# Output projection of a decoder layer: columns 0 to 1023 as seven block products of quarters, columns 1024 to 2047 first, token sums made beside those

## The chip, the core and the metric

The kernel runs on one core of one Trainium2 chip. The time is device microseconds (us) of one execution. The kernel before took 1541.53 us (median of 3 runs, 1541.39 to 1544.05). One execution was profiled; all rows below come from it.

Five engines matter. PE multiplies matrices; each matmul here holds a 128x128 block (the stationary operand, loaded just ahead of it) and streams the other operand past it into a PSUM bank, 512 columns wide or 256. DVE and ACT work element by element, on SBUF and on PSUM. SP and POOL issue transfers; a transfer that POOL issues may add to what lies in SBUF already. Each engine takes its instructions in the order in which the program lists them for it, and waits at the head of that list until what the instruction needs is there.

## The reference, cut to what matters

```python
x: (1, 512, 2048) f32;  w_out: (2048, 2048) f32
merged = sigmoid(g_mla) * y_mla + sigmoid(g_sgu) * y_sgu      # (1, 512, 2048)
x = x + gate[:, None] * (merged @ w_out)                      # one output projection
return rmsnorm(x, final_norm_g)                               # over the 2048 columns of a token
```

Everything ahead of these lines (adaLN, the input projection, attention over 16 heads, the spatial gating unit) is the same in both kernels.

## The kernel before, in words

All products are made in three matmuls: each f32 operand is cut into a high part (rounded to the matmul's f32r format) and a low part (the rest), and a product is high x high + high x low + low x high (`mm3`, L185 to L187; `block` and `out_block` do the same).

`merged` lies transposed in SBUF as 16 chunks of 128 channels x 512 tokens, in high and low parts, `mh[j]` and `ml[j]` (tiles `b0` to `b15` and `g0` to `g15`). `w_out` is cut into four column groups of 512 (cg 0 to 3) and each of these into 8 granules of 256 channels (`wo[cg, i]`, a tile of 128 x 1024, 512 KB).

A `Stream` (`ws`) brings the granules, in the order of its list:
- `dma_to` has SP load a granule into one of three raw tiles, `wraw0` to `wraw2`, and holds back when all three are held; a raw tile is given back when its granule has been split.
- `cast_to` has ACT copy it into a high tile (L139, `w0h` or `w1h`); `split_to` has DVE subtract the high part from the raw one into a low tile (L151, `w0l` or `w1l`). A high and a low tile of a granule can be overwritten only when PE has done the granule two places earlier.
- `get(i)` is called at the start of a step: it puts the cast and the split of granule i+1 on the lists of ACT and DVE, and returns granule i. What a step does besides stands behind them on the same lists.

The output projection is a row of 32 such steps. The first three (cg 0, i = 0 to 2) are worked in between the parts of attention's last head. A step (`out_granule`) is 24 matmuls of 512 columns: 2 chunks x 4 token blocks of 128 x 3. The four token blocks of a column group lie in four PSUM banks; the next group takes the other four. When a group is done, `residual` runs for its four token blocks, one per `get`: DVE multiplies by the gate row (`grow`) and adds the input (`yt`), ACT squares the row into a sum (L1838), DVE multiplies by the final norm's gain (`gfb`).

In cg 2, each `get` also brings a granule of cg 3 into tiles of its own (`dh`, `dl`), so that at the end cg 3 can be worked token block by token block: 48 matmuls of 512 columns for each of the first three blocks, and for the last one 48 of 256 columns twice. Each block's row is finished and stored while the next is multiplied: sum of squares, square root (ACT L1869), reciprocal, scale, four stores of 256 KB.

Earlier stages of the same kernel make two other projections as seven products of quarters in place of eight (`block`, L701, for 512, 384 or 320 columns; and L1502 to L1504). There, sums of weights are made by transfers that add (`onto`, L284, `transfer`, L866) or by DVE.

Of the kernel before, what the change touches and what calls it, by code (L numbers as in the profile page):

```python
# [20 lines left out]
P = 128  # L21
D = 2048
# [143 lines left out]
def trunk_layer(ctx, tc, xT, xn, c, vecs, pos, wada, w1, w2, wv, wv3, wv4, wh, wh15, wq, wqr, wk, wvv, wo, wsT, bsp, gfin, out,  # L166
# [188 lines left out]
    dlast = []  # L355

    def last_tiles():
        k = len(dlast)
        dlast.append((nt(dp[0].p, [P, GW], F32R, f"dh{k}"), nt(dp[0].p, [P, GW], F32R, f"dl{k}")))
        return dlast[-1]  # L360

    go = {}
    for cg in range(3):
        for i in range(8):
            go[cg, i] = ws.add(wo[cg, i], GW)
            if cg == 2 and i < 6:
                go[3, i] = ws.add(wo[3, i], GW, to=last_tiles)
    for i in (6, 7):
        go[3, i] = ws.add(wo[3, i], GW)
# [551 lines left out]
    for s in range(n_slots):  # L921
        def both(s=s):
# [5 lines left out]
        on(s - 2, SPLIT, both)  # L928
# [840 lines left out]
    def out_granule(cg, i, banks, ahead=1):  # L1769
        wH, wL = get(go[cg, i], ahead)  # L1770
# [7 lines left out]
    for h in range(H):  # L1778
# [5 lines left out]
        first = go[0, 0] if not more else gr[pair] if not odd and 2 * pair < H else None  # L1784
# [6 lines left out]
        else:  # L1791
            pso = [bank_at(k) for k in range(NB)]
            for i in range(2):
                out_granule(0, i, pso)
# [3 lines left out]
        if more:  # L1798
            kps = kproj(h + 1)
            kfinish(h + 1, kps)  # L1800
        else:
            merge()
            out_granule(0, 2, pso)
# [18 lines left out]
    grow = nt(dp[0].p, [P, D], F32, "gbc")  # L1822
    gfb = nt(dp[0].p, [P, D], F32, "gfb")
    yt = nt(dp[0].p, [P, NB, D], F32, "y")
    load_before(go[0, 7], lambda: (DMA.dma_start(grow, bcast(gate_row, D)), DMA.dma_start(gfb, bcast(gfin, D))))
    for n in range(NB):
        load_before(go[1, n], lambda n: DMA.dma_start(yt[:, n], xn[n]), n)
    ssy = nt(dp[0].p, [P, NB, 5], F32, "ssy")
    ry = nt(dp[0].p, [P, 12], F32, "ry")

    def residual(n, part, sl, ps, last=False):
        y = yt[:, n, sl]
        w = sl.stop - sl.start
        t = nt(tp, [P, S], F32, "sig", bufs=3)[:, :w]
        tt(t, ps, grow[:, sl], ALU.mult)
        tt(y, t, y, ALU.add)
        junk = nt(tp, [P, S], F32, "sig", bufs=3)[:, :w]
        ACT.activation(junk, y, AF.Square, accum_out=ssy[:, n, part:part + 1])  # L1838
        if not last:
            tt(y, y, gfb[:, sl], ALU.mult)  # L1840

    for cg in range(3):
        if cg > 0:
            pso = [bank_at((4 * cg + k) % 8) for k in range(NB)]
# [107 lines left out]
```

## Time and profile before

| | |
|---|---|
| median of 3 runs | 1541.53 us |
| the profiled execution | 1542.18 us, of which the span from its first to its last instruction is 1540.5 us |
| granted TensorE clock, mean | 0.999 |
| matmuls in the program | 10533 |
| ACT's cast in the first step of cg 1 / of cg 2 starts at | 1401.16 us / 1444.68 us |
| last matmul starts at | 1532.04 us |
| transfers that add, all before 1056 us | 58.2 MB in 111 of 512 or 384 KB and some small ones |

The page's first part gives for each engine its busy time and share of the span. The timeline lists instructions in order of time: start, duration, engine, line, operation, output<-inputs, shape, and in brackets how long the engine sat idle before it and what ended that. A matmul's duration is its way through the array; the next one starts before it is over.

### The profile page before, as it was taken

How to read it: one execution, taken by the hardware profiler on the slowest of the kernel's cores; microseconds unless marked ns; L12 is line 12 of the kernel's file. 1: busy time of each engine (PE TensorE's matmuls, PEld its weight loads, DVE VectorE, ACT ScalarE, POOL GpSimd, SP SyncE). 2: the span in 40 equal slices, each digit the busy share in tenths (PEclk: the TensorE clock that was granted, in tenths of full speed). 3: DMA queues.
4: the chain of work that ended last, by engine and by line, in shares of the span. 5: the costliest groups of instructions: out<-in, count | busy, mean ns of one | idle time of the engine just before them, and what ended most of it. 6: DMA issues, size and time to landing. Idle time of an engine off the chain costs nothing.

```text
span 1540.5 us, 27351 instructions
## 1 busy us (share of the span) xinstructions
PE 1527.4 (99%) x10632; PEld 1423.8 (92%) x10632; DVE 1194.3 (78%) x1856; ACT 784.8 (51%) x1379; POOL 112.0 (7%) x136
## 2 busy tenths in 40 slices
PE   9999999999999999999999999999999999999997
PEld 7888988999999999999999999999888888888886
DVE  8989988768888888877777777778788888854543
ACT  4444566555555454454546546456555555632322
POOL 0000011011111111111101111120000000000000
PEclk9999999999999999999999999999999999999999
DMA  9978699778999998998888888887544443245423
GB/s 376 389 270 313 194 266 295 226 210 235 283 248 268 276 252 255 262 240 231 216 239 248 216 244 242 217 200 209 175 131 134 127 138 133 89 164 181 139 80 110
DMA packets 134868, 335.97 MB, mean 218 GB/s; under 512 B 15417, under 2 KB 39761, under 8 KB 130001
## 3 DMA queue, kind: packets, MB, share of 16 engines
q1 hardware_dynamic: 116434, 275.76, 51.8%
q0 software_dynamic: 18160, 58.20, 20.8%
q8 instruction: 83, 1.36, 0.3%
q14 instruction: 47, 0.39, 0.1%
q10 hardware_dynamic: 144, 0.26, 0.0%
HBM read 310.24 MB, written 23.94 MB: 217 GB/s over the span
## 4 chain that ended last, share of the span: by engine, by line
PE 94%; DMA 3%; ACT 1%; DVE 1%; issue 1%; SPq 0%; DVEq 0%; ACTq 0%; POOL 0%; POOLq 0%
PE ps L1502 15%; PE ps L1503 15%; PE ps L1504 15%; PE ps L186 12%; PE ps L185 12%; PE ps L187 12%; PE ps L701 7%; PE ps L1681 1%; DMA wraw<-in_wv 1%; PE ps L1062 1%; DMA wraw<-in_w 1%; PE ps L1645 1%; PE ps L1644 1%; DMA half<-in_pos 0%; DMA raw<-in_wv 0%
## 5 line engine op out<-in xcount | busy, mean ns | idle before, releaser
L1502 PE MATMUL ps<-h,w0h 128*128 128x256 f32 x408 | 113.1, 277 | 0.9 <-DVE lat L173 0.9
L1502 PE MATMUL ps<-h,w2h 128*128 128x256 f32 x408 | 113.8, 279 | 0.0
L1504 PE MATMUL ps<-h,w0l 128*128 128x256 f32 x408 | 112.7, 276 | 0.0
L1503 PE MATMUL ps<-h,w0h 128*128 128x256 f32 x408 | 112.7, 276 | 0.0
L1504 PE MATMUL ps<-h,w2l 128*128 128x256 f32 x408 | 112.7, 276 | 0.0
L1503 PE MATMUL ps<-h,w2h 128*128 128x256 f32 x408 | 112.7, 276 | 0.0
L1502 PE MATMUL ps<-h,w1h 128*128 128x256 f32 x400 | 110.9, 277 | 0.0
L1504 PE MATMUL ps<-h,w1l 128*128 128x256 f32 x400 | 110.5, 276 | 0.0
L1503 PE MATMUL ps<-h,w1h 128*128 128x256 f32 x400 | 110.5, 276 | 0.0
L139 ACT CAST w0h<-wraw 128x1024 fp32r<-128x1024 f32 (+5 forms) x67 | 59.1, 889 | 73.3 <-PE ps L187 25.3
L151 DVE TENSOR_TENSOR w0l<-wraw,w0h 128x1024 fp32r<-128x1024 f32 (+5 forms) x61 | 63.7, 1047 | 38.6 <-ACT w0h L139 38.1
L173 DVE TENSOR_TENSOR w0l<-raw,w0h 128x1024 fp32r<-128x1024 f32 x56 | 68.5, 1224 | 31.2 <-ACT w0h L888 30.4
L139 ACT CAST w1h<-wraw 128x1024 fp32r<-128x1024 f32 (+5 forms) x67 | 53.9, 811 | 72.4 <-PE ps L187 25.0
L151 DVE TENSOR_TENSOR w1l<-wraw,w1h 128x1024 fp32r<-128x1024 f32 (+5 forms) x63 | 59.1, 943 | 36.9 <-ACT w1h L139 33.9
L185 PE MATMUL ps<-h,w1h 128*128 128x512 f32 x218 | 86.6, 397 | 0.0
L186 PE MATMUL ps<-h,w1h 128*128 128x512 f32 x218 | 85.1, 390 | 0.0
L187 PE MATMUL ps<-h,w1l 128*128 128x512 f32 x218 | 85.0, 390 | 0.0
L173 DVE TENSOR_TENSOR w1l<-wraw,w1h 128x1024 fp32r<-128x1024 f32 x44 | 53.9, 1225 | 36.4 <-ACT w1h L888 36.4
L173 DVE TENSOR_TENSOR w2l<-wraw,w2h 128x1024 fp32r<-128x1024 f32 x46 | 56.3, 1224 | 30.2 <-ACT w2h L888 30.2
L185 PE MATMUL ps<-h,w0h 128*128 128x512 f32 x198 | 78.1, 394 | 0.0
L186 PE MATMUL ps<-h,w0h 128*128 128x512 f32 x198 | 77.3, 390 | 0.5 <-DVE h L176 0.5
L1502 PEld LDWEIGHTS ps<-h,w0h 128*128 128x128 f32 x408 | 76.6, 188 | 1.0 <-issue 1.0
(419 smaller groups left out, 5461.6 us busy)
## 6 DMA issues: line engine op xcount, KB each, us to landing
raw<-in_wh SPq DMA_DIRECT2D x104, 512.0 KB, 6.9
wada<-in_wada SPq DMA_DIRECT2D x31, 1024.0 KB, 7.7
wraw<-in_wh POOLq DMA_DIRECT2D x55, 512.0 KB, 8.3
wraw<-in_wh SPq DMA_DIRECT2D x44, 512.0 KB, 6.4
raw<-in_wh POOLq DMA_DIRECT2D x36, 512.0 KB, 7.4
wraw<-in_wo SPq DMA_DIRECT2D x32, 512.0 KB, 3.6
half<-in_w SPq DMA_DIRECT2D x35, 256.0 KB, 5.4
wraw<-in_w SPq DMA_DIRECT2D x16, 512.0 KB, 8.4
```

The lines of the kernel that those rows point to most:

```text
L139: self.nc.scalar.copy(self.hi[k][0][:, sl], src)
L151: self.nc.vector.tensor_tensor(out=lo[:, sl], in0=src, in1=hi[:, sl].bitcast(F32), op=ALU.subtract)
L173: DVE.tensor_tensor(out=out, in0=in0, in1=in1, op=op)
L185: PE.matmul(ps, ah, bh, start=start, stop=False)
L186: PE.matmul(ps, ah, bl, start=False, stop=False)
L187: PE.matmul(ps, al, bh, start=False, stop=stop)
L701: PE.matmul(psv[key][n], x_[:, tk], w_[:, sl], start=st and m == 0, stop=ch == 7 and m == 2, skip_group_check=True)
L1062: PE.matmul(ps[:, n], v[:, n], wr[:, q], start=True, stop=True)
L1502: PE.matmul(ps[:, :256], wH[:, cols[c]], xh, start=c == 0 and first, stop=False, skip_group_check=True)
L1503: PE.matmul(ps[:, :256], wH[:, cols[c]], xl, start=False, stop=False, skip_group_check=True)
L1504: PE.matmul(ps[:, :256], wL[:, cols[c]], xh, start=False, stop=c == 7, skip_group_check=True)
L1644: PE.matmul(ps, q2[:, q], krh[:, :n], start=False, stop=False)
```

## The change

Columns 1024 to 2047 (cg 2, then cg 3) now come first, in 16 steps as before (steps 0 to 15 below). Columns 0 to 1023 and the 512 tokens and 2048 channels are cut in halves each way, and the eight products of quarters are replaced by seven, named "1" to "7". Each is 8 chunks x 2 token blocks x 3 = 48 matmuls of 512 columns, in four steps of 12 (`out_block`):

| steps | product | stationary: tokens | weights: quarters of `wo[0]`, `wo[1]` |
|---|---|---|---|
| 16 to 19 | "1" | `mh`, left half | `wo[1, i]`, loaded |
| 20 to 23 | "6" | V, right half | `wo[0, i]` + `wo[1, i]`, added by a transfer in tile `ch` |
| 24 to 27 | "7" | V, left half | `wo[1, 4+i]`, loaded |
| 28 to 31 | "2" | U, left half | `wo[1, 4+i]` added onto `ch` |
| 32 to 35 | "3" | U, right half | `wo[1, i]` loaded, `wo[1, 4+i]` added onto it |
| 36 to 39 | "4" | `mh` of chunks 8 to 15, right half | `wo[0, 4+i]` added onto `ch` |
| then | "5" | `mh` of chunks 8 to 15, left half | `wo[0, 4+i]`, loaded; token blocks 0 and 1, the second in two halves of 256 columns |

(The signs and the exact quarters are those of the code; a granule's number in a tile's name is 144 + step, so `w1h_162` is step 18.)

- The token sums U and V are made by `out_sums(j)`, one per step, at steps 4 to 7 and 12 to 15: two DVE additions of 512 columns, four subtractions or additions of 256, an ACT copy and a DVE subtraction for V's high and low part. `split_u(j)` cuts U into high and low parts at steps 18 to 23.
- Products share two pairs of banks: "1", "2", "3", "4" add up in y; "6" and "7" in z. Between them, ACT copies a bank out (`hold`, L1889): z after step 23, y after steps 31 and 35. The four corners of the result are put together by DVE from these copies (`difference`, `corner_row`, `c11`, `c21`).
- `plain_row` is the old `residual` for cg 2 (steps 8 to 11) and cg 3 (steps 16, 17, 26, 27); the multiplication by the gain stands apart (`weigh`).
- From step 18 the stream has a third high tile (`w2h`) and casts two granules ahead; the low tiles stay two. From step 16 it looks seven granules ahead for loads.
- Rows 2 and 3 are finished by `row_out` (two ACT multiplications of 1024 columns, two stores of 512 KB), rows 0 and 1 by the old end.

The diff, cut to what is spoken of:

```diff
+    def chain_out(i):
+        chain[i] = t = nt(dp[0].p, [P, GW], F32, f"ch{i}")
+        DMA.dma_start(t, wo[0, i])
+    go = {(cg, i): ws.add(wo[cg, i], GW) for cg in (2, 3) for i in range(8)}
+    for p in "1672345":
+        for i in range(2 if p == "5" else 0, 4):
...
+            elif p == "3":
+                g = ws.add(wo[1, i], GW, fetch=lambda t, i=i: both(t, wo[1, 4 + i]))
+            elif p == "6":
+                g = ws.add(None, GW, fetch=lambda t, i=i: [chain[i][:, :]])
+            else:
+                src, by = wo[int(p == "2"), 4 + i], go["6" if p == "2" else "2", i]
+                g = ws.add(None, GW, fetch=lambda t, i=i, src=src: chain_add(i, src, GW), after=by)
...
+    def out_sums(j):
...
+        tt(u, mh[j].bitcast(F32), ml[j].bitcast(F32), ALU.add)
+        tt(v, mh[j + 8].bitcast(F32), ml[j + 8].bitcast(F32), ALU.add)
+        tt(v[:, right], u[:, right], v[:, right], ALU.subtract)
+        tt(u[:, right], u[:, left], u[:, right], ALU.subtract)
+        tt(u[:, left], v[:, right], u[:, left], ALU.subtract)
+        tt(v[:, left], u[:, left], v[:, left], ALU.add)
+        V[j] = nt(dpp, [P, 2, S], F32R, f"V{j}")
+        hilo(V[j][:, 0], V[j][:, 1], v)
...
+    def hold(name, n, ps, pl, tag):
+        held[name, n] = t = nt(pl, [P, S], F32, tag, bufs=3 if tag == "sig" else 1)
+        ACT.copy(t, ps)
...
+    for n in range(2):
+        at_out(23, lambda n=n: hold("z6", n, pbank["z"][n], dpp, f"k{n}"))
+        at_out(31, lambda n=n: hold("y12", n, pbank["y"][n], tp, "sig"))
+        at_out(35, lambda n=n: hold("y123", n, pbank["y"][n], tp, "sig"))
+    for j in range(8):
+        at_out((4, 5, 6, 7, 12, 13, 14, 15)[j], out_sums, j)
+        at_out((18, 18, 19, 19, 20, 21, 22, 23)[j], split_u, j)
+    for n in range(NB):
+        at_out(8 + n, plain_row, n, 2)
+        at_out((16, 17, 26, 27)[n], plain_row, n, 3)
...
+        if s == 16:
+            ws.look = 7
+        if s == 18:
+            a, b = ws.next_hi, 1 - ws.next_hi
+            ws.his, ws.next_hi = [(dpp, "w2h", 0, 0), ws.his[a], ws.his[b]], 0
...
+            w = get(seq[s], cast=seq[s + 2] if s >= 18 else None)
...
+                out_block(p, i, n, w, pbank[key][n])
+        for f in todo.pop(s, ()):
+            f()
```

**How it moves instructions, place one: ACT around step 16.** Before, at the same place (the start of cg 2) ACT's list has two casts in a row, then a square (`w0h_162` is the granule two steps on, `dh1` one of cg 3):

```order
L139 CAST dh0_2005_16497<-wraw1_161_16407 128x1024
L139 CAST w0h_162_16501<-wraw2_162_16437 128x1024
L1838 ACTIVATE sig_2008_16512,ssy_1987_16067<-y_1986_16066 128x512
L139 CAST dh1_2009_16539<-wraw0_163_16467 128x1024
L139 CAST w1h_164_16543<-wraw1_164_16505 128x1024
```

Now, from step 13's `get` to step 18's (V5 to V7 are the high parts of token sums, `ps4` and `ps5` the squares of `plain_row`, `b0` the high part of a split U):

```order
L139 CAST w1h_158_16464<-wraw1_158_16353 128x1024
L190 CAST V5_2018_16501<-sig_2017_16494 128x512
L139 CAST w0h_159_16505<-wraw2_159_16390 128x1024
L190 CAST V6_2021_16543<-sig_2020_16536 128x512
L139 CAST w1h_160_16547<-wraw0_160_16426 128x1024
L190 CAST V7_2023_16584<-sig_2022_16577 128x512
L139 CAST w0h_161_16588<-wraw1_161_16468 128x1024
L1896 ACTIVATE ps4_2002_16270,ssy_1984_16064<-yp_1991_16071 128x512
L139 CAST w1h_162_16612<-wraw2_162_16509 128x1024
L1896 ACTIVATE ps5_2003_16271,ssy_1984_16064<-yp_1991_16071 128x512
L139 CAST w2h_163_16634<-wraw0_163_16551 128x1024
L139 CAST w0h_164_16638<-ch0_2006_16278 128x1024
```

Between two casts there now stands one instruction that needs DVE's work of the step before.

**Place two: POOL and ACT around steps 32 to 37.** Before, POOL issues nothing in the output projection. Now its list ends with 16 transfers that add; the last eight are those of steps 32 to 39:

```order
L284 DMA wraw2_176_16788<-in_wo 128x1024
L284 DMA wraw0_177_16814<-in_wo 128x1024
L284 DMA wraw1_178_16836<-in_wo 128x1024
L284 DMA wraw2_179_16933<-in_wo 128x1024
L284 DMA ch0_2006_16278<-in_wo 128x1024
L284 DMA ch1_2008_16314<-in_wo 128x1024
L284 DMA ch2_2010_16351<-in_wo 128x1024
L284 DMA ch3_2012_16388<-in_wo 128x1024
```

`wraw2` serves step 32 (176) and again step 35 (179), so the load and the added transfer of 179 come after the split of 176, and those onto `ch0` to `ch3` stand behind them on POOL. ACT's list at steps 33 to 37 (`sig_2064`, `sig_2065` are the copies of the y banks after step 35):

```order
L139 CAST w0h_179_16986<-wraw2_179_16933 128x1024
L1896 ACTIVATE ps4_2036_16690,ssy_1984_16064<-ys0_2040_16708 128x512
L139 CAST w1h_180_17007<-ch0_2006_16278 128x1024
L1896 ACTIVATE ps5_2037_16691,ssy_1984_16064<-ys1_2041_16710 128x512
L139 CAST w2h_181_17026<-ch1_2008_16314 128x1024
L1889 COPY sig_2064_17040<-ps0_2024_16594 128x512
L1889 COPY sig_2065_17042<-ps1_2025_16595 128x512
L139 CAST w0h_182_17048<-ch2_2010_16351 128x1024
```

The copies of the y banks, which step 36 writes next, now stand behind the cast of step 37's granule.

**Place three: ACT at the end.** Before, between the square of row 2 and the two half squares of row 3 stand a square root and one multiplication of 512 columns, both of row 2. Now, behind the square of row 0 (`sig_2074`), two multiplications of row 3 stand ahead of the half squares of row 1 (`sig_2075`, `sig_2076`):

```order
L1896 ACTIVATE sig_2074_17169,ssy_1984_16064<-ys0_2040_16708 128x512
L2026 ACTIVATE ry_1985_16065<-ssy_1984_16064,ry_1985_16065 128x1
L2034 ACTIVATE yp_1991_16071<-yp_1991_16071,ry_1985_16065 128x512
L1947 ACTIVATE yp_1991_16071<-yp_1991_16071,ry_1985_16065 128x1024
L1947 ACTIVATE ys3_2063_16980<-ys3_2063_16980,ry_1985_16065 128x1024
L1896 ACTIVATE sig_2075_17212,ssy_1984_16064<-ys1_2041_16710 128x256
L1896 ACTIVATE sig_2076_17243,ssy_1984_16064<-ys1_2041_16710 128x256
```

More of the change, by code (lines that the diff above doesn't have):

```diff
@@ L1842, in trunk_layer @@
[L1842 to L1851 removed]
+    dpp = dp[0].p
+    ssy = nt(dpp, [P, NB, 5], F32, "ssy")
```

223 lines of the change are left out of this document (158 added, 65 removed).

## The prediction, made before the changed kernel was run

> **What bounds the kernel now.** I read the page's busy times first, then the chain that ended last, then who PE waited for.
>
> ```profile
> span 1540.5 us, 27351 instructions
> PE 1527.4 (99%) x10632; PEld 1423.8 (92%) x10632; DVE 1194.3 (78%) x1856; ACT 784.8 (51%) x1379; POOL 112.0 (7%) x136
> PE 94%; DMA 3%; ACT 1%; DVE 1%; issue 1%; SPq 0%; DVEq 0%; ACTq 0%; POOL 0%; POOLq 0%
> PE ps L701 <- DVE w1l L151: 1.4, 1, 1.4
> 1444.40:1532.30 87.90, 87.90 (x434) 74.59 (x432) 44.14 (x67) 27.14 (x45) 0.00 (x0) 1.00 0.32 108
> ```
>
> PE has no room: 94% of the closing chain is matmuls, and the longest of its waits on other work is 1.4 us, for one split. The last row is the stretch from cg 2 to the last matmul: PE busy throughout, DVE 44.14 and ACT 27.14 of 87.9 us. So fewer matmuls shorten the kernel as long as DVE, ACT and the transfers keep up. By their totals they would. The question is the order.
>
> **What goes: matmuls.** Not the mean duration counts but the distance between starts:
>
> ```profile
> 1505.00 0.39 PE L185 MATMUL ps<-dh,b 128*128 128x512 f32 x1
> 1520.42 0.39 PE L187 MATMUL ps<-w0h,g 128*128 128x512 f32 x1
> 1520.64 0.28 PE L185 MATMUL ps<-dh,b 128*128 128x256 f32 x1
> 1532.04 0.28 PE L187 MATMUL ps<-w0h,g 128*128 128x256 f32 x1
> ```
>
> From the first to the second lie 68 distances: 15.42/68 = 0.227 us. From the third to the fourth 95: 11.40/95 = 0.120 us. Before: 720 matmuls of 512 columns and 96 of 256; after: 384 + 288 + 24 = 696 and 48. Gone are 24 x 0.227 + 48 x 0.120 = **-11.2 us**. (By the durations, 0.39 and 0.28, it would look like some 23.) A step of 24 takes 5.44 us, one of 12 takes 2.72.
>
> **What comes, first term: ACT's line at steps 12 to 19.** Durations of the pieces:
>
> ```profile
> 1401.16 1.05 ACT L139 CAST w0h<-wraw 128x1024 fp32r<-128x1024 f32 x1 [4.38 <-PE ps L187]
> 1402.25 1.23 DVE L151 TENSOR_TENSOR w0l<-wraw,w0h 128x1024 fp32r<-128x1024 f32 x1 [4.22 <-ACT w0h L139]
> 1403.39 0.68 DVE L173 TENSOR_TENSOR sig<-ps,gbc 128x512 f32<-128x512 f32 x1
> 1404.11 0.69 DVE L173 TENSOR_TENSOR y<-sig,y 128x512 f32<-128x512 f32 x1
> 1404.83 0.63 ACT L1838 ACTIVATE sig<-y 128x512 f32<-128x512 f32 x1 [2.62 <-DVE y L173]
> 1448.36 0.63 ACT L1838 ACTIVATE sig<-y 128x512 f32<-128x512 f32 x1 [2.62 <-DVE y L173]
> 1448.99 1.03 ACT L139 CAST dh<-wraw 128x1024 fp32r<-128x1024 f32 x1
> 1344.62 0.68 DVE L151 TENSOR_TENSOR w0l<-wraw,w0h 128x512 fp32r<-128x512 f32 x1
> 1345.23 1.49 DVE L173 TENSOR_TENSOR lat<-ps,lat 128x512 fp32r<-128x512 f32 x3
> 194.98 0.42 DVE L173 TENSOR_TENSOR x<-x,x 128x256 f32<-128x256 f32 x1
> 195.43 0.42 DVE L173 TENSOR_TENSOR x<-x 128x256 f32<-128x256 f32 x1
> 1532.81 0.43 DVE L173 TENSOR_TENSOR y<-sig,y 128x256 f32<-128x256 f32 x1
> 1533.27 0.42 ACT L1838 ACTIVATE sig<-y 128x256 f32<-128x256 f32 x1 [5.25 <-DVE y L173]
> 1370.72 0.62 ACT L190 CAST b<-sig 128x512 fp32r<-128x512 f32 x1 [1.36 <-DVE sig L173]
> 1371.24 1.05 ACT L139 CAST w0h<-wraw 128x1024 fp32r<-128x1024 f32 x1
> ```
>
> From start to start: cast to split 1.09, split to the next DVE operation 1.14, 512 columns to a dependent operation 0.72, to an independent one 0.61, 256 columns to a dependent one 0.45 (to ACT 0.46), ACT's cast of 512 to its next 0.52, its square to its next cast 0.63.
>
> With token sums (steps 12 to 15) one turn is: split 1.14, first sum 0.61, second 0.72, three of 256 columns 1.35, the fourth and over to ACT 0.46, high part of V 0.52, next cast and over to DVE 1.09: 5.89 us, against a step of 5.44. The cast of step s+1 stands behind the high part of V, so the turn runs 0.45 us late per step. A nominal split starts 1.29 us into a step (the cast 0.2 in, 1.09 more). Step 12's is nominal; three turns on, that of step 15 starts 2.64 in, and step 16's (granule 17) 3.09 in. PE wants that low part at 2.72 + 0.23 = 2.95; it is there at 3.09 + 1.23 + 0.03 = 4.35: PE waits 1.4. In steps 16 and 17 the turn is split 1.14, `plain_row` 0.72 + 0.72, square 0.63, cast 1.09 = 4.30 us, but a PE step that starts on its low part takes 2.72: 1.58 more, twice. Then the casts run two ahead and nothing of this stands between. **+4.5 us.** If nothing is late at step 16, 2.9 remain. Steps 4 to 7 run late in the same way, but steps of 5.44 us follow and take it up.
>
> **Second term: steps 24 and 32.** A copy of z's second bank starts 0.2 into step 24; behind it on ACT stands the high part of the last U (0.52 on), for which DVE waits (0.65), and then come `weigh` (0.61), the next operation (0.61) and only then the split of granule 25: start 2.59, there at 3.85 against 2.95: **+0.9 us**. At step 32 the same with a cast of 1024: the split of 33 is there at 4.2, +1.3; this one is counted in the next term.
>
> **Third term: steps 31 to 36, a raw tile that comes free late.**
>
> ```profile
> wraw<-in_wo SPq DMA_DIRECT2D x32, 512.0 KB, 3.6
> raw<-in_wh POOLq DMA_DIRECT2D x36, 512.0 KB, 7.4
> 205.78 1.88 POOL L284 DMA_DIRECT2D raw<-in_wv  x2 [196.11 <-DMA raw<-in_wv]
> 209.25 0.85 POOL L284 DMA_DIRECT2D raw<-in_wv  x1 [0.18 <-issue]
> DMA to landing us min/median/max: 9.2/12.0/14.5
> 308.03 0.84 POOL L284 DMA_DIRECT2D raw<-in_wv  x1 [5.37 <-DVE w0l L151]
> 310.11 0.85 POOL L284 DMA_DIRECT2D raw<-in_wv  x1 [1.24 <-DVE w1l L151]
> DMA to landing us min/median/max: 4.8/5.0/5.1
> ```
>
> Let R be the start of step 31. Granule 35 needs the raw tile of 32, whose split ends at R + 1.9. Its load lands 3.6 later (R + 5.5), and only then may POOL add the second quarter; the transfers of granules 36 to 39 wait behind that on POOL. An added transfer takes a. In the rows: 7.4 in the median of a busy stage; 9.2 to 14.5 for a burst of four issued from 205.78 to 209.25, beside other traffic; 4.8 to 5.1 for one from 308.03 on. I take a = 7.4, as loads run beside it here as well. The first burst, issued within 3.5 us, landed from 215.0 to 223.75, so g = 8.75/3 = 2.9 us apart. Granule 37 then lands at R + 5.5 + a + 2g. ACT's cast of it (0.96 to the next) stands ahead of the copy of the y banks (0.6), which PE's step 36 waits for: R + 7.05 + a + 2g, where R + 13.6 is nominal. So the delay is a + 2g - 6.55 = 7.4 + 5.8 - 6.55 = **+6.65 us**. At a = 4.8 and g = 0.85 (POOL's own time for one) the step 35 wait decides: a - 3.3 = 1.5. At a = 12.0 it is 11.3.
>
> The Trainium skill weighs against this, in "DMA: Bandwidth & Descriptors", section "Anatomy of one DMA — SWDGE (gpsimd) path": a transfer issued by POOL takes about 2.0 us + bytes/436e3. By that, 512 KB take 3.2 us; the third term would shrink to step 32's 1.3, and the sum to about -1.7 us. The rows here are of transfers that add and show 4.8 to 14.5, so I go by them.
>
> **Fourth term: the end.**
>
> ```profile
> 1504.23 1.28 ACT L1869 ACT_TABLE_LOAD   x1
> 1509.96 0.69 DVE L173 TENSOR_TENSOR sig<-ps,gbc 128x512 f32<-128x512 f32 x1 [2.11 <-PE ps L187]
> 1514.16 0.15 DVE L1866 TENSOR_REDUCE ry<-ssy 128x1 f32<-128x3 f32 x1
> 1506.05 0.73 ACT L1876 ACTIVATE y<-y,ry 128x512 f32<-128x512 f32 x1 [0.23 <-DVE ry L1870]
> 1534.34 0.51 ACT L1874 ACTIVATE y<-y,ry 128x256 f32<-128x256 f32 x1 [0.23 <-DVE ry L1870]
> 1532.35 0.42 DVE L173 TENSOR_TENSOR sig<-ps,gbc 128x256 f32<-128x256 f32 x1 [3.62 <-PE ps L187]
> ```
>
> Before, DVE took up the last half row at 1532.35, at once after PE. Now let X be DVE's start on row 0. As in rows 1509.96 to 1514.16, it is through with that row at X + 4.2; then comes the reciprocal of row 3 (0.2), then ACT's two multiplications of 1024 columns: 0.73 for 512 and 0.51 for 256 make 1.17 for 1024, 2.25 for both. Behind them stands the square of row 1's first half (0.6), then on DVE `weigh`, reduce, scale (0.75): X + 8.0. PE is done with that half at X + 48 x 0.120 = X + 5.8: 2.2 late. X itself is some 0.6 late, since the table load for the square root now follows the last `c21`. **+2.8 us**, between 0 (ACT is through in time) and 4.
>
> At no cost I count the token sums of steps 4 to 7, the second column group's rows and the earlier added transfers: PE's 5.44 us steps and eight steps of lead cover them. The stores at the end are as many bytes as before.
>
> **The sum**: -11.2 + 4.5 + 0.9 + 6.65 + 2.8 = +3.65 us. From the profiled execution, 1542.18, that is 1545.9; it stands 0.65 above the median of the runs shown, so **1545.2 us**.
>
> **Rivals.**
> - *Added transfers land quickly* (a 4.8, g 0.85): -11.2 + 4.5 + 0.9 + 1.5 + 2.8 = -1.5, 1540.0 us. For it: the burst of 4.8 to 5.1. Against: those were 384 KB and issued 2 us apart. Chance 0.22.
> - *Faster: ACT's order does not hold casts back.* If a cast starts when its own inputs are there, the first two terms go, step 36 waits for nothing, step 35 still waits a - 3.3 = 4.1, and the end keeps 0.6: -11.2 + 4.7 = -6.5, 1535.0 us. It decides if the first and fourth term together stay under 4 us. Against it: at 1371.24 a cast began just behind the cast of `b` that had waited for DVE. Chance 0.16.
> - *Crowded transfers* (a 12.0): +8.3, 1549.8 us. Chance 0.14. PE would then sit idle over 5 us in one piece.
> - *The matmuls are not saved*: the program lists 10461 matmuls after 10533, 72 fewer, as counted. Chance 0.02.
>
> ```profile
> 1534.00:1536.00 2.00, 0.00 (x0) 0.00 (x0) 1.44 (x4) 1.23 (x3) 0.00 (x0) 1.00 0.12 44
> 1536.00:1538.00 2.00, 0.00 (x0) 0.00 (x0) 0.00 (x0) 0.00 (x0) 0.00 (x0) 0.78 1.05 376
> ```
>
> Here the granted clock was still 1.00 up to 3.7 us after the last matmul and 0.78 in the 2 us after that. The forecast's longest gap is about 2.5 us, so no clock is lost in it. The Trainium skill ("TensorE: Matmul & The Clock Gate", section "The HAM clock gate (the "warmup" mystery)") has the clock halved after an idle window of about 3.4 us and for as long a busy one after it. The trace agrees; under the crowded rival it would add about 1.7 us, an estimate from that page.
>
> **How the numbers follow.** The forecast keeps 0.46, mostly between 1542 and 1549. Leaving out the lower half of the faster rival, the upper half of the crowded one and the last, the range is 1535 to 1551. A measurement of this kernel tells about 0.2% (3.1 us) from no change: the forecast lies just beyond (slower 0.28, same 0.18), the quick rival mostly inside. Together: faster 0.18, same 0.37, slower 0.45.
>
> **What would show it.** PE waits of about 1.4 to 1.6 us at the low tiles of granules 161, 162 and 163 (L151), each with ACT's square just ahead of the cast; a wait near granule 179 for the cast, and one at step 36 for the copy L1889 with `ch1` landing just ahead; the last half row taken up 2 to 3 us after the last matmul. If PE runs through steps 16 to 19 without a wait, the first term is wrong. If granule 179 lands within 5 us of POOL's issue, the third is.

## The result, and the profile of the changed kernel

| | median | runs | ratio to before, 95% interval |
|---|---|---|---|
| before | 1544.05 us | 5 (1541.39 to 1547.02) | |
| changed | 1553.06 us | 5 (1552.29 to 1555.50) | 1.0063 (1.0045 to 1.0081) |
| changed, again, beside other runs | 1554.32 us | 5 (1553.14 to 1556.12) | 1.0068 (1.0055 to 1.0082) |

The change costs about 10 us. Slower was right, the size was not: the prediction had +3.65 us, and the time lies above its range.

First the page of the changed kernel: span, busy times, and the chain that ended last by engine.

```profile
span 1551.0 us, 27409 instructions
PE 1523.9 (98%) x10560; PEld 1417.0 (91%) x10560; DVE 1243.0 (80%) x1934; ACT 810.2 (52%) x1415; POOL 125.3 (8%) x152
PE 90%; DVE 4%; DMA 3%; ACT 2%; issue 1%; POOL 0%; SPq 0%; DVEq 0%; ACTq 0%; POOLq 0%
```

Matmuls were 94% of the closing chain and are 90%; DVE went from 1% to 4%. PE's busy time fell by only 3.5 us, though 72 matmuls are gone: some of the others took longer. The next view gives the three longest of PE's waits from 1400 us on (who waited, for what, total, times, longest), the one after it cuts three parts out of the last stretch (PE, PEld, DVE, ACT, POOL busy, then the granted clock, DMA share, GB/s).

```profile
PE ps L1881 <- ACT sig L1889: 6.3, 1, 6.3
PE ps L1881 <- DVE w0l L151: 4.1, 5, 1.1
PE ps L1881 <- DVE sig L173: 2.8, 1, 2.8
```

```profile
1506.00:1514.00 8.00, 1.67 (x7) 1.13 (x6) 3.41 (x4) 3.69 (x6) 0.00 (x0) 0.86 1.05 273
1514.00:1519.00 5.00, 5.00 (x14) 3.85 (x14) 1.77 (x4) 1.15 (x2) 0.00 (x0) 0.55 0.64 141
1536.00:1543.00 7.00, 4.64 (x24) 4.43 (x24) 3.30 (x11) 3.31 (x5) 0.00 (x0) 0.76 0.96 372
```

From 1514 to 1519 PE is busy all the time and yet does 14 matmuls where 22 fit: the clock is 0.55. The same shows from 1536 to 1543. So two things are to be read from PE's timeline: where it waits, and how far apart its matmuls start. Here are PE's rows at the first wait, at the longest and at the last:

```profile
1447.11 0.50 PE L1881 MATMUL ps<-w0h,b 128*128 128x512 f32 x1 [0.33 <-ACT w0h L139]
1448.37 0.50 PE L1881 MATMUL ps<-w0l,b 128*128 128x512 f32 x1 [0.76 <-DVE w0l L151]
...
1506.80 0.39 PE L1881 MATMUL ps<-w0h,g 128*128 128x512 f32 x1
1513.53 0.79 PE L1881 MATMUL ps<-w1h,b 128*128 128x512 f32 x1 [6.33 <-ACT sig L1889]
1514.12 0.63 PE L1881 MATMUL ps<-w1l,b 128*128 128x512 f32 x1
1514.54 0.63 PE L1881 MATMUL ps<-w1h,g 128*128 128x512 f32 x1
...
1535.09 0.28 PE L1881 MATMUL ps<-V,g 128*128 128x256 f32 x1
1538.12 0.50 PE L1881 MATMUL ps<-V,b 128*128 128x256 f32 x2 [2.75 <-DVE sig L173]
```

A matmul of 512 columns starts 0.227 us after the one before it. What a distance has beyond that is lost. From 1506.80 to 1513.53 that is 6.73 - 0.23 = 6.50 us, a little more than the 6.33 that the bracket gives. Behind it the matmuls start 0.43 us apart, twice the usual. ACT's rows ahead of step 18 show the order that the first term is about: the cast of granule 162 starts only behind a square, and the square had waited for DVE.

```profile
1449.67 0.60 ACT L1896 ACTIVATE ps<-yp 128x512 f32<-128x512 f32 x1 [2.62 <-DVE yp L173]
1450.30 1.03 ACT L139 CAST w1h<-wraw 128x1024 fp32r<-128x1024 f32 x1
```

All distances in the last stretch, added up in this way, make the ledger:

| term | predicted | in the profile |
|---|---|---|
| 72 matmuls fewer | -11.2 | -11.2 |
| first: waits in steps 17, 18 and 19 | +4.5 | 1.63 + 1.49 + 1.52 = +4.64 |
| second: low part of granule 169 | +0.9 | +0.98 |
| third: granules 177 and 179, then the stop ahead of step 36 | +6.65 | 1.34 + 1.51 + 6.50 = +9.35 |
| slow matmuls behind that stop | none | +2.40 |
| fourth: the end | +2.8 | stop of 2.91 between the halves of product 5 |
| slow matmuls behind that stop | none | +1.6 |
| sum | +3.65 | +10.7 |

Executions differ by some us in the stages far ahead of the change (why, see the end). So I compare the profiles from one DVE row that stands at the same place in all of them; in the changed kernel it is this one:

```profile
1344.02 0.68 DVE L151 TENSOR_TENSOR w0l<-wraw,w0h 128x512 fp32r<-128x512 f32 x1
```

From its start to the end of the span are 1551.0 - 1344.02 = 206.98 us; before, with the row quoted in the prediction, 1540.5 - 1344.62 = 195.88. The difference is 11.1 us; the ledger has 10.7, and the rest lies in distances a few hundredths too long. Below this stretch is called **the tail**. A second profile of the changed kernel (e11) has 206.4 us, so two profiles of one kernel can differ by 0.6 us in it.

Last, DVE's, POOL's and ACT's rows for the third term (the first is the split of granule 176), and the DMA queues from 1456 to 1518 (packets, MB, share of sixteen engines' time; q0 is POOL's, q1 the loads of SP):

```profile
1491.17 1.22 DVE L151 TENSOR_TENSOR w1l<-wraw,w0h 128x1024 fp32r<-128x1024 f32 x1
1496.46 0.84 POOL L284 DMA_DIRECT2D wraw<-in_wo  x1 [8.00 <-DVE V L173]
1496.99 3.80 POOL L284 DMA_DIRECT2D ch<-in_wo  x4
```

```profile
1502.04 1.05 ACT L139 CAST w0h<-wraw 128x1024 fp32r<-128x1024 f32 x1 [6.13 <-DMA wraw<-in_wo]
1508.11 1.04 ACT L139 CAST w1h<-ch 128x1024 fp32r<-128x1024 f32 x1 [4.39 <-DMA ch<-in_wo]
1511.94 1.04 ACT L139 CAST w2h<-ch 128x1024 fp32r<-128x1024 f32 x1 [2.16 <-DMA ch<-in_wo]
1512.89 1.06 ACT L1889 COPY sig<-ps 128x512 f32<-128x512 f32 x2
```

```profile
q0 software_dynamic: 1728, 6.29, 54.4%
q1 hardware_dynamic: 2016, 7.34, 34.5%
```

The split of 176 ends at 1492.4 and gives the raw tile back; SP issues the load of 179 into it at 1492.46, and that lands at 1495.9. POOL issues the added transfer of 179 at 1496.46 and the four onto `ch` at once behind it. (The bracket names a subtraction of DVE because that ended last, at 1496.24; POOL's list stood still until the load had landed.) Each cast starts when its transfer lands: granule 179 after 5.6 us, 180 after 6.07 more, 181 after 3.83 more. The copies that PE's step 36 waits for stand behind the cast of 181, as the order had shown. The queue rows give a price: twelve added transfers took 0.544 x 62 = 33.7 us of all sixteen engines, 2.80 each; fourteen plain ones 21.4 us, 1.53 each.

### The profile page after: what moved, and what is told of

Its sections match the earlier page's. It is cut to its first block, busy times and chain, and to the rows that moved or that the text cites. A ratio compares the mean times of both kernels' runs of the same rounds, so it can differ in the third digit from the quotient of the medians.

```text
span 1551.0 us, 27409 instructions
## 1 busy us (share of the span) xinstructions
PE 1523.9 (98%) x10560; PEld 1417.0 (91%) x10560; DVE 1243.0 (80%) x1934; ACT 810.2 (52%) x1415; POOL 125.3 (8%) x152
## 4 chain that ended last, share of the span: by engine, by line
PE 90%; DVE 4%; DMA 3%; ACT 2%; issue 1%; POOL 0%; SPq 0%; DVEq 0%; ACTq 0%; POOLq 0%
PE ps L1509 15%; PE ps L1511 15%; PE ps L1510 15%; PE ps L185 10%; PE ps L186 10%; PE ps L187 10%; PE ps L708 7%; PE ps L1881 3%; PE ps L1688 1%; DMA ch<-in_wo 1%; DMA wraw<-in_wv 1%; PE ps L1069 1%; DMA raw<-in_wh 1%; DVE w0l L151 1%; PE ps L1652 1%
## 5 line engine op out<-in xcount | busy, mean ns | idle before, releaser
L873 POOL DMA_DIRECT2D wraw<-in_wh x55 | 49.2, 951 | 368.1 <-DVE w1l L173 163.5
L187 PE MATMUL ps<-h,w0l 128*128 128x512 f32 x198 | 77.4, 391 | 0.0
L1509 PEld LDWEIGHTS ps<-h,w2h 128*128 128x128 f32 x408 | 76.6, 188 | 0.5 <-issue 0.5
```

Of the source, the lines that this page charges most:

```text
L187: PE.matmul(ps, al, bh, start=False, stop=stop)
L873: q_.dma_start(t, wh[h, n, q // 10 - 1], **eng)
L1509: PE.matmul(ps[:, :256], wH[:, cols[c]], xh, start=c == 0 and first, stop=False, skip_group_check=True)
```

## The experiments

The theories: **A**, the third stop comes from POOL being held behind granule 179, whose raw tile comes free late. **B**, the DMA engines are full there, and the bytes set the time. **D**, the last stop is a shared PSUM bank. **F**, the slow matmuls follow from PE's own idle time. The rivals stand in the expectations. The times carry the spread of the early stages, some 4 us, as much as most of these edits do; so the verdicts rest on the profiles, and the ratios are there to compare. All kernels keep the line numbers of the changed one. The tail of each, worked out as above:

| run | edit | ratio to before | tail |
|---|---|---|---|
| before / changed / changed again | | 1 / 1.0063 / 1.0068 | 195.9 / 207.0 / 206.4 |
| e1 | rows 2 and 3 loaded later | 1.0073 (1.0054 to 1.0091) | 205.8 |
| e2 | a tile of its own for granule 179 | 1.0036 (1.0016 to 1.0056) | 198.3 |
| e3 | transfers write, do not add | 1.0043 (1.0026 to 1.0060) | 198.5 |
| e4 | casts two ahead from step 12 | 1.0050 (1.0035 to 1.0065) | 201.2 |
| e5 | third bank for product 5 | one time, 1551.79 us | 205.3 |
| e6 | third bank, ACT's end spread | 1.0064 (1.0046 to 1.0083) | 205.4 |
| e7 | e1, e2, e4, e6 together | 0.9976 (0.9963 to 0.9990) | 194.6 |
| e8 | e7, splits earlier | 0.9966 (0.9950 to 0.9981) | 189.6 |
| e9 | PE kept busy, one piece | 1.0084 (1.0071 to 1.0097) | 206.4 |
| e10 | e8, row 2 out early | 0.9952 (0.9939 to 0.9965) | 188.9 |
| e12 | PE kept busy, two pieces | 1.0058 (1.0044 to 1.0072) | 203.6 |

### e1: the rows out of the way

```diff
-        ys[n] = nt(dpp, [P, GW], F32, f"ys{n}")
+        ys[n] = nt(dpp, [P, GW], F32, f"ys{n}" if n < 2 else f"ch{n - 2}")
...
-        at_out((20, 20, 32, 32)[n], row_load, n)
+        at_out((20, 20, 36, 37)[n], row_load, n)
```

> Edit: the two loads of the input rows of token blocks 2 and 3 (512 KB each) no longer start beside the last added transfers; they go into the tiles of ch0 and ch1 and so wait for the splits of granules 36 and 37. Theory A (late release: POOL stands behind granule 35's added transfer, whose tile comes free late): the rows do not matter for the release; ch1 lands within 0.5 us of where it did, PE's wait at step 36 stays above 6 us and its slow matmuls stay; 1552 to 1554 us. Theory B (full DMA engines: in the profile of the change they are at 0.96 to 1.06 from 1500 to 1516, and a plain transfer takes 21.4/14 = 1.53 us of all sixteen): 3.1 us of transfer time leave the queue ahead of ch1; the wait at step 36 falls from 6.5 to about 3.4 us, and the 2.4 us of slow matmuls behind it may go; 1547.6 to 1550 us.

ACT's casts of 179 and 181 in this run:

```profile
1506.81 1.05 ACT L139 CAST w0h<-wraw 128x1024 fp32r<-128x1024 f32 x1 [6.29 <-DMA wraw<-in_wo]
1515.58 1.04 ACT L139 CAST w2h<-ch 128x1024 fp32r<-128x1024 f32 x1 [1.14 <-DMA ch<-in_wo]
```

They lie 8.77 us apart where it was 9.90, and the stop ahead of step 36 is 5.35 us (distances) where it was 6.50. Between the theories: of the 3.1 us that B takes out, 1.1 come back at this place; the transfers run side by side, so only a part of the rows' work lay ahead of `ch1`. The tail is 1.2 us shorter, which the times can't tell.

### e2: a tile of its own for granule 179

```diff
+    own = lambda: (DMA.dma_start(t := nt(dp[0].p, [P, GW], F32, "V7"), wo[1, 3]), [t[:, :]])[1]
...
-                g = ws.add(wo[1, i], GW, fetch=lambda t, i=i: both(t, wo[1, 4 + i]))
+                g = ws.add(wo[1, i] if i < 3 else None, GW, fetch=lambda t, i=i: both(t or own(), wo[1, 4 + i]), after=-1 if i < 3 else go["2", 1])
```

> Edit: granule 35 is loaded into the tile of V7, which is free from step 28 on, in place of the raw tile of granule 32. Theory A: its load starts at about the start of step 28 and POOL is past it some 8 us earlier; ch1 lands about 8 us earlier, the waits at step 35 (1.5 us) and step 36 (6.5 us and 2.4 us of slow matmuls) go; 1553.1 - 10.4 = 1542.7 us. Theory B: the engines had only 4.2 us idle from 1488 to 1500 (shares 0.85, 0.57, 0.54 of 4 us each); ch1 lands about 4.2 us earlier, some 2.3 us of the wait at step 36 stay; about 1546 us. In both the wait of 1.3 us at step 33 stays.

Here the whole list of PE's waits from 1490 to 1525 us, and POOL's two rows:

```profile
PE ps L1881 <- DVE w0l L151: 1.1, 1, 1.1
```

```profile
1493.38 0.84 POOL L284 DMA_DIRECT2D V<-in_wo  x1 [3.45 <-DMA V<-in_wo]
1493.92 3.81 POOL L284 DMA_DIRECT2D ch<-in_wo  x4
```

The waits for 179 and ahead of step 36 are gone but for 0.3 us of long distances; the one at 177 stays, as it should. This execution is 4.05 us late from the front (the mark is at 1348.07), so POOL's 1493.92 is 1489.9 on the first kernel's clock, 7.1 us earlier, and ACT's cast of 181 starts 7.8 us earlier (1508.21 here), where A has about 8 and B 4.2. The tail is 8.7 us shorter: 10.1 us of stop and slow matmuls went, 1.3 came back at the last stop (3.50 us, and 2.3 us of slow matmuls). A decides: the same bytes, released earlier, are in time. The median, 1548.19 us, is above both expectations; the lateness from the front is part of it.

### e3: writing in place of adding

```diff
-        nc.gpsimd.dma_start(t, src, accum_op=ALU.add)
+        nc.gpsimd.dma_start(t, src, **({} if ws.look == 7 else dict(accum_op=ALU.add)))
```

> Edit: the twelve transfers that POOL issues from step 16 on write instead of adding (the addition of the quarters is left out there). In the profile of the change an added transfer takes 33.7/12 = 2.80 us of all sixteen DMA engines, a plain one 1.53. If this price sets the spacing of the landings (theories A and B alike, behind the release): granules 36 and 37 land 1.27 us closer together each, ch1 about 3.8 us earlier, the wait at step 36 falls to about 2.7 us or less and the slow matmuls go; 1543 to 1547 us. If it is a fixed cost of a transfer issued by POOL, whatever it does (theory C): spacing 3.8 us as before, no change; 1552 to 1554 us.

POOL issued 179's transfer at 1501.63 here; the casts:

```profile
1505.50 1.05 ACT L139 CAST w0h<-wraw 128x1024 fp32r<-128x1024 f32 x1 [4.40 <-DMA wraw<-in_wo]
1508.53 1.05 ACT L139 CAST w1h<-ch 128x1024 fp32r<-128x1024 f32 x1 [1.35 <-DMA ch<-in_wo]
1511.05 1.04 ACT L139 CAST w2h<-ch 128x1024 fp32r<-128x1024 f32 x1 [0.85 <-DMA ch<-in_wo]
```

Landing after 3.9 us (5.6 with adding), then 3.03 and 2.52 apart (6.07 and 3.83). The stop ahead of step 36 is 1.97 us, and nothing is slow behind it; the tail is 8.4 us shorter (the median, 1550.13 us, shows less: the profiled execution is 5.1 us late at the mark). The queue rows say the same: from 1461 to 1521 us the twelve transfers of POOL take 30.0% of sixteen engines' time, 1.50 us each, and the fourteen plain loads 34.8%, 1.49 each. So it is the adding that makes these transfers slow, not that POOL issues them; C falls.

### e4: casts two ahead from step 12

```diff
-        if s == 18:
+        if s == 12:
...
-            out_granule(2 + s // 8, s % 8, pso[s // 8])
+            out_granule(2 + s // 8, s % 8, pso[s // 8], seq[s + 2] if s >= 12 else None)
...
-            w = get(seq[s], cast=seq[s + 2] if s >= 18 else None)
+            w = get(seq[s], cast=seq[s + 2])
```

> Edit: the third high-part tile is taken from step 12 on and not from step 18, and the casts run two steps ahead from there. First term's theory (the cast stands behind the high part of V and the squares on ACT): the waits in the steps 16 to 19 (1.63 + 1.49 + 1.52 = 4.64 us) fall below 1 us together; everything behind moves up, the added transfers too; 1548.5 to 1549.5 us. If the DMA engines set the time of steps 35 and 36 (theory B), PE arrives earlier and waits longer there: step 36's wait grows by what was won, 1552 to 1554 us.

PE's waits from 1400 to 1500 us, the whole list:

```profile
PE ps L1881 <- DVE w0l L151: 2.5, 3, 1.1
PE ps L1881 <- ACT w0h L139: 0.2, 1, 0.2
```

The four that are left are those of 169, 177 and 179; steps 16 to 19 have none. Step 36's stop is 6.46 us as before: the transfers moved up with the work, since they are released by it. The tail is 5.8 us shorter, the first term's 4.64 and some slow matmuls. The first term is shown.

### e5 and e6: the end

```diff
-    pso = [bank_at(2 + k) for k in range(2)]
+    pso = [bank_at(2 + k) for k in (0, 1, 4)]
...
-        ps = pso[n]
         for part, (o, w) in enumerate(((0, S),) if n == 0 else ((0, half), (half, half))):
+            ps = pso[n + part]
```

> Edit: the second half of token block 1 in product 5 gets a PSUM bank of its own. In the profile of the change PE stopped for 2.9 us between the two halves, until DVE's first reading of the first half, and its next matmuls ran at half clock for some 1.5 us. Theory D (the halves share a bank, so PE may not write it before DVE has read): the stop and the slow matmuls go, PE ends about 2.9 us after the first half; DVE still reads the first half late and weighs it before it takes up the second, so of the end only about 1.7 us are won. Theory E (PE waits there for something that DVE does late, whatever the bank): the stop stays, nothing is won.

PE runs from the first half to the second without a stop and at full clock; its last matmul starts at 1538.42. DVE takes the second half up only behind the weighing of the first, 2.7 us after PE's last matmul has ended (1538.70):

```profile
1541.44 0.41 DVE L173 TENSOR_TENSOR sig<-ps,gbc 128x256 f32<-128x256 f32 x1
```

The tail is 1.7 us shorter, as expected: D holds. The Trainium skill says why the wait must be there ("PSUM — Partial Sum Buffer", section "PSUM bank collisions raise a hardware error"): two engines may not be in one bank at the same time, so a program has to keep them apart. The 2.75 us in PE's row are what that costs here.

e6 spreads ACT's multiplications too (`row_out(n, k)` is now one of the two halves; row 3's second goes to DVE):

```diff
-    row_out(2)
+    DVE.reciprocal(out=ry[:, 2:4], in_=ry[:, 2:4]), row_out(2, 0)
...
-            if not last:
-                weigh(ys[n][:, sl], sl)
+            if n:
+                weigh(ys[n][:, :o], slice(0, o)) if last else row_out(3, 0)
-        ACT.activation(r, ssy[:, n, 3 + part:4 + part], AF.Sqrt, bias=r, scale=1.0 / D)
+        ACT.activation(r, ssy[:, n, 3 + part:4 + part], AF.Sqrt, bias=r, scale=1.0 / D), n and row_out(3, 1, True)
...
-            row_out(3)
+            row_out(2, 1)
```

> Edit: the bank of its own, and on ACT the multiplications of rows 2 and 3 are spread: the first ahead of row 0's square, the next behind row 0, the next behind the first half's square, the last on DVE beside the last square root; the first half is weighed behind the second's sums. Theory D with ACT's order (the fourth term): DVE takes up the last half row at most 1 us after PE is done with it, the end comes about 3.6 us earlier than in the changed kernel; ratio to before 1.0040 in place of 1.0063. If the stores of rows 0, 2 and 3, bunched closer to the end, set the end (rival): the last half row is taken up as early, but the end gains 1 to 2 us only; ratio 1.0050 to 1.0057.

DVE's row for the second half, and the DMA engines behind it:

```profile
1540.67 0.41 DVE L173 TENSOR_TENSOR sig<-ps,gbc 128x256 f32<-128x256 f32 x1
```

```profile
1542.00:1546.00 4.00, 0.00 (x0) 0.00 (x0) 1.90 (x5) 1.50 (x4) 0.00 (x0) 0.79 1.02 402
```

PE's last matmul ended at 1539.95, DVE is 0.7 us behind. Yet the end comes 10.0 us after this row, where it was 8.2: the stores had been pushed together, 402 GB/s at a share of 1.02, and SP's last two issues take 1.15 and 1.16 us, in the changed kernel 0.38 and 0.40. The tail is 1.6 us shorter, no more than in e5, as the rival had it.

### e7, e8, e10: the mends together

e7 is e1, e2, e4 and e6 in one kernel.

> Edit: rows late, granule 35 in V7's tile, casts two ahead from step 12, and the tail of the run before, together. If the four causes are independent: waits of steps 16 to 19 (4.6 us), of steps 35 and 36 with the slow matmuls (10.4 us) and 3.6 us of the end go: 18.6 us less than the changed kernel, ratio to before 1.0063 - 18.6/1542 = 0.9942. If the DMA engines are next in line (theory B: PE reaches step 36 some 4.6 us earlier while the added transfers have the same work ahead of them): 2 to 4.6 us of wait come back at steps 34 to 37, ratio 0.9955 to 0.9972.

The list of PE's waits from 1440 to 1530 us in e7:

```profile
PE ps L1881 <- ACT sig L1889: 3.0, 1, 3.0
PE ps L1881 <- DVE w0l L151: 1.8, 2, 1.1
```

B's share comes back: 3.11 us of stop and 1.7 of slow matmuls at step 36, and the stores of e6. The ratio, 0.9976, lies above both expectations, with an interval that reaches into B's. The tail is 12.4 us shorter than the changed kernel's; 18.6 - 4.8 - 2.0 = 11.8 is what the expectation leaves. e8 moves the splits that stood ahead of others:

```diff
-        at_out((18, 18, 19, 19, 20, 21, 22, 23)[j], split_u, j)
+        at_out((18, 18, 19, 19, 20, 20, 21, 22)[j], split_u, j)
-        at_out(30 + n, early_split, n)
+        at_out(28 + n, early_split, n)
```

> Edit: as the run before, and the splits of U for j = 5 to 7 and of the two early granules of product 5 are made one or two steps earlier, so that at steps 24 and 32 no high part stands between the copies of a bank and the next split. Second term's theory: the waits of 0.98 us at granule 169 and 1.34 us at granule 177 go; 2.3 us less than the run before, ratio 0.0015 lower. Rival: DVE's line is as long as PE's there and the same wait shows one or two steps away; no difference beyond 0.0005.

```profile
PE ps L1881 <- DVE w1l L151: 0.3, 1, 0.3
PE ps L1881 <- DVE w0l L151: 0.3, 1, 0.3
```

These are all of PE's waits from 1400 to 1525 us in e8. Of the second term's 2.3 us, 1.2 are still there, as two waits two or three steps away, so the rival has half; but step 36's stop went as well, and the tail is 5.0 us shorter than e7's. POOL is through with 178 and 179 some 2.4 us earlier, measured from the mark, presumably because the splits that give the raw tiles back come earlier; that was not tried by itself. e10 puts row 2 out early again:

```diff
-    DVE.reciprocal(out=ry[:, 2:4], in_=ry[:, 2:4]), row_out(2, 0)
+    DVE.reciprocal(out=ry[:, 2:4], in_=ry[:, 2:4]), row_out(2, 0), row_out(2, 1)
...
-            row_out(2, 1)
+            pass
```

> Edit: the run with the earlier splits, but both multiplications and stores of row 2 come before row 0's square again (one of row 2's stores starts some 5 us earlier). If the bunched stores set the end (in that run the last half row was taken up 10.0 us ahead of the end, in the changed kernel 8.2): the half row is taken up 0.5 to 1.2 us later, the end comes up to 2 us earlier. If the chain through DVE and ACT sets it: the end is 0.5 to 1.2 us later.

```profile
span 1533.8 us, 27413 instructions
```

DVE takes the last half row up 9.1 us ahead of the end, where it was 10.0 in e8, and the tail is 0.7 us shorter; that is within what runs differ. But e10 as a whole, 0.9952 (0.9939 to 0.9965), is **faster than both kernels**: some 7 us, or 0.5%, under the one before. Its tail is 7.0 us shorter than that kernel's, not 11.2: PE still loses 1.4 us to waits, and from the start of the last matmul to the end are 11.0 us where it was 8.5. The seven products are worth their 11.2 us only when nobody is late.

### e9, e12: the slow matmuls

e9 is the changed kernel with matmuls added whose result nobody reads, at the places where PE stopped; e11 is the changed kernel again.

```diff
+    fill = lambda w, n, m, b: [PE.matmul(b[:, :m], mh[15][:, :P], w[:, :m], start=True, stop=True) for _ in range(n)]
...
-            p, i = "167234"[s // 4 - 4], s % 4
+            p, i = "167234"[s // 4 - 4], s % 4; s == 36 and fill(w[0], 26, S, bank_at(7))
...
-                weigh(ys[n][:, sl], sl)
+                weigh(ys[n][:, sl], sl); fill(wl[0][0], 20, half, bank_at(7))
```

> Edit: the changed kernel, and PE is kept busy where it stopped: 26 matmuls of 512 columns (5.9 us) into a bank that nobody reads ahead of step 36, and 20 of 256 columns (2.4 us) between the halves of token block 1; nothing waits for them. Theory F (the granted clock falls because PE stands still for most of one of its 3.41 us windows): the clock stays at 1.00 at both places, a step-36 matmul starts every 0.227 us again and not every 0.427, and the 2.4 + 1.5 to 1.7 us of slow matmuls go; the waits themselves (6.5 and 2.9 us until the copy and until DVE's reading) stay; about 4 us less than the changed kernel. Theory G (the clock follows something else at that time, such as the full DMA engines at 1.06 or the kernel's end): the same windows are granted 0.50, no difference, or up to 1 us more.

> The changed kernel itself, beside the two others, for a comparison on one chip: ratio to before 1.0063 within 0.002; waits of 1.5 us at granules 161 to 163, a stop of 5 to 7 us at step 36 with slow matmuls behind it, a stop of 2.9 us in product 5.

The time says nothing for e9: in it and in e11 the long stop fell into two pieces (2.6 to 2.7 us ahead of step 35 and, in e11, 2.8 ahead of step 36; with the slow matmuls behind them e11 loses 9.9 us at steps 35 and 36, the first profile 10.4), so 5.9 us of filling were too many ahead of step 36 and held it up by about 3 us. But e9's windows tell the theories apart:

```profile
1510.00:1514.00 4.00, 3.68 (x10) 2.90 (x11) 2.72 (x5) 1.67 (x3) 0.00 (x0) 0.59 1.06 274
1518.00:1520.00 2.00, 2.00 (x11) 1.65 (x9) 1.08 (x2) 0.00 (x0) 0.00 (x0) 1.00 1.09 225
```

Behind the piece that was not filled the clock is 0.59; in the filled one it is 1.00 with the DMA engines just as full. G falls. e12 shares the filling out.

```diff
+            p, i = "167234"[s // 4 - 4], s % 4; s in (35, 36) and fill(w[0], 14 if s == 35 else 16, S, bank_at(7))
```

> Edit: the changed kernel with the filling matmuls shared out: 14 of 512 columns (3.2 us) ahead of step 35, 16 (3.6 us) ahead of step 36, 20 of 256 columns (2.4 us) between the halves. From the end of step 34 to the copy that step 36 waits for were 10.8 us in the profile of the change and 10.9 in the repeat of it; 2.7 us of that is step 35's own work and 6.8 us are filled, so the filling should not hold step 36 up. Theory F: the clock is 1.00 from step 33 to the end of product 5; no matmul starts 0.427 us after the one before it; the slow matmuls' 3.9 to 4.8 us go and the rest stays; some 3.5 to 4 us less than the changed kernel, ratio to before 1.0040 to 1.0046 against its 1.0068 on this chip. If the slow clock only ran in the shadow of the transfers, so that PE would wait for them as much longer: the clock is 1.00 and the time is the changed kernel's, 1.0060 to 1.0070.

```profile
1510.00:1514.00 4.00, 3.39 (x15) 2.46 (x14) 2.43 (x3) 1.90 (x4) 0.00 (x0) 1.00 1.05 272
1534.00:1538.00 4.00, 3.65 (x31) 3.45 (x30) 2.52 (x7) 2.81 (x6) 0.00 (x0) 1.00 0.90 348
```

No slow matmul is left, and the tail is 2.8 us shorter than e11's (203.6 for 206.4), with 50 matmuls more. By the ratios it is 0.0010 less, within their intervals; and e12 ran on another chip than e11, each beside its own runs of the kernel before. F holds for the clock; of the 3.5 to 4 us, the profile shows 2.8.

## Why the prediction was wrong

**The matmuls saved**: right. The distances are 0.227 and 0.120 us again.

**First term**: right in mechanism, place and size (4.64 for 4.5): squares just ahead of the casts, waits at the low tiles of 161 to 163, and e4 takes them away.

**Second term**: right, 0.98 for 0.9; at granule 177, 1.34 for the 1.3 that the third term counts.

**Third term**: the chain was right: raw tile, POOL's order, the cast ahead of the copies; and e2 shows that the late tile is the cause. Put into its formula, the landing times of the profile (a = 5.6, g = (1511.94 - 1502.04)/2 = 4.95) give 5.6 + 9.9 - 6.55 = 8.95, against 9.35 in PE's rows. The step that failed is "g = 8.75/3 = 2.9 us apart". Between the landings of 179 and 181, from 1502 to 1511.9 us, the two queues took of all sixteen engines:

```profile
q0 software_dynamic: 343, 1.27, 65.3%
q1 hardware_dynamic: 377, 1.35, 37.6%
```

That is 3.2 us a landing for POOL's queue and 1.9 for SP's, from which four plain loads of 512 KB, issued from 1497.4 to 1499.7, ran among the added ones. I had counted them as traffic that a = 7.4 covers, and not between the landings. The burst that g was taken from had plain loads beside it too, but fewer: from 215 to 223.75 us of the kernel before the queues took 79.4% and 27.8%, so 2.3 and 0.8 us a landing. Plain loads thus make up about half of the 2.0 us that g was short; why POOL's own part is larger here as well is open. e3 shows the price of the adding (2.8 apart without it), e1 that of the rows (about 0.55 of 4.95). a was too high by 1.8, which hid part of the miss.

**The clock**: the larger miss, 4.0 of 7 us. "The forecast's longest gap is about 2.5 us, so no clock is lost in it" was wrong twice. The gap at step 36 became 6.5 us, because a short and g long put most of the delay into one piece; and no gap of 3.4 us is needed: 2.75 us of waiting was enough at the end. e12 has both stops filled and no slow matmul.

**Fourth term**: that 2.91 is so near to 2.8 is luck, for it is another wait. I had PE done early and DVE late on the last half row, behind ACT's two multiplications. But both halves lie in one bank, so PE may start the second only when DVE has read the first, and DVE takes the last half up at once when PE is done:

```profile
1537.66 0.41 DVE L173 TENSOR_TENSOR sig<-ps,gbc 128x256 f32<-128x256 f32 x1
1542.80 0.42 DVE L173 TENSOR_TENSOR sig<-ps,gbc 128x256 f32<-128x256 f32 x1 [1.72 <-PE ps L1881]
```

That first reading stands behind row 0's chain, at X + 4.8 (X = 1532.89). The lateness that was worked out is there too: DVE is through with the first half's weighing and sums at 1541.08, X + 8.2 for X + 8.0; but PE, stopped and then slow, was later still. e5, with a bank more, brings out the wait as it was forecast, 2.7 us for 2.8. So the chain through ACT and DVE was right, and the shared bank was left out; it costs 1.7 us of the tail on top. This step I had not read out of the diff: the old end took a new bank for each half.

**The rivals**: "added transfers land quickly" and the Trainium skill's formula ("DMA: Bandwidth & Descriptors", section "Anatomy of one DMA — SWDGE (gpsimd) path"; 3.2 us for 512 KB) come nearer to what e3 shows for transfers that only write (3.9 us, then 2.5 to 3.0 apart); for those that add the rows say 5.6 us and 3.8 to 6.1 apart. "Faster" fell with the first term. "Crowded transfers", at 1549.8 us with a chance of 0.14, came nearest, and it had the clock loss with it; but its a = 12.0 is not what happened (5.6), so its number is near by luck.

## What to carry to other kernels

Here a stop of PE that took up more than half of a 3.4 us window cost its own length and then one window or more of matmuls at half clock (2.4 us lost behind the stop of 6.5, 1.6 behind that of 2.9): in a kernel that PE bounds, a forecast has to add it, and ask where one wait collects what several would have shared. A change that saves work on the bounding engine is worth its saving only if tiles, banks and the order on the helping engines keep up; here a handful of local mends turned +10 us into -7. The spacing of a burst of transfers is a price for that burst's company; in another stage, add the engine time of every load that runs among them.

## What the runs showed of the hardware that I had not expected

**The clock goes by windows.** In the trace's record of the granted clock, the changes in the changed kernel come at 1511.71, 1518.54, 1539.02 and 1542.43 us: all whole multiples of 3.41 apart, in the other runs as well. I compared PE's idle time in the 3.41 us ahead of each boundary with the clock behind it. With 1.69 us idle (e6, at 220 to 223 us) or less the clock stayed at 1.00; with 1.73 (e9, at 217 to 220 us), 1.82 (e3), 1.87 (e5), 2.18 (e7) or more it was halved for the next window. Once halved, 0.52 us of idle (e2, at 224 to 228 us) or less let it come back, 0.71 and 0.82 (e5) did not; there the slow clock lasted four windows. In the fourteen profiles, some 6300 windows, none goes the other way. "TensorE: Matmul & The Clock Gate" in the Trainium skill (section "The HAM clock gate (the "warmup" mystery)") has the same free-running window of 3.41 us, but speaks of an idle window; here half of one is enough.

**A part of what makes executions differ is the same thing.** The profiles of e1, e2, e3 and e9 are 3.6 to 5.1 us late at the mark, long before the change. Most of it, 3.2 to 3.9 us, arises from 217 to 228 us, behind a burst of four added transfers that both kernels have. The added ones land no more than 0.1 us later there than in the changed kernel's profile. What lands late is a plain load of SP, issued near 203 us: at 217.1 to 219.3 us in these four, at 215.1 in the changed kernel. ACT's cast has to wait for it, here in e3, then the same cast in the changed kernel:

```profile
219.44 1.14 ACT L139 CAST w1h<-wraw 128x512 fp32r<-128x512 f32 x2 [7.00 <-DMA wraw<-in_wv]
```

```profile
215.19 1.14 ACT L139 CAST w1h<-wraw 128x512 fp32r<-128x512 f32 x2 [3.13 <-PE ps L708]
```

PE waits with it and crosses the line of half a window. These are e3's windows; in the changed kernel the clock is 1.00 in both:

```profile
218.00:222.00 4.00, 1.92 (x8) 1.17 (x7) 1.89 (x3) 2.02 (x5) 0.00 (x0) 0.99 1.06 223
222.00:226.00 4.00, 3.43 (x9) 2.15 (x7) 0.94 (x2) 3.02 (x8) 0.00 (x0) 0.58 0.94 295
```

Set beside the changed kernel's profile matmul by matmul, the halved window makes up 0.9 to 1.6 us of the 3.2 to 3.9, the late load the rest. Why that load lands later in some executions is open.
